# Softmax over rows of 512: the last two rows of the sixth tile's groups are loaded through GpSimd's DMA queue

## The chip, the cores and the metric

The kernel runs on one core of one Trainium2 chip. The metric is the device time in microseconds of an execution; of the kernel before there are three runs, 162.20, 162.28 and 162.33 us, median 162.28.

## The reference

The input x has 16 x 1024 rows of 512 float32 numbers. Each row is divided by a temperature of 0.5 and put through a softmax:

```python
x_scaled = x / temp                         # temp = 0.5
x_max = np.max(x_scaled, axis=-1, keepdims=True)
exp_x = np.exp(x_scaled - x_max)
return (exp_x / np.sum(exp_x, axis=-1, keepdims=True)).astype(np.float32)
```

33.55 MB are read and as many written.

## The kernel before, in words

The 16,384 rows are cut into C = 8 tiles of 128 partitions with G = 16 consecutive rows on each, so a partition's share of a tile is 32 KB, contiguous in HBM and in SBUF. There are six buffers for the tiles (BUFS); tile 6 goes into the buffer of tile 0 and tile 7 into that of tile 1. The exponentials and the products are written over the tile itself.

The order of the work is written out by hand (`manual_schedule`). The lists LOADS, BLOCKS and STORES (lines 38 to 40) say in which pieces a tile is loaded, computed and stored. Tile 0 is loaded in two pieces (four rows and twelve) and computed in three blocks (4, 4 and 8 rows), tile 7 is computed in two blocks of 8, and all others are loaded, computed and stored whole.

For a block, `shift` has VectorE take the negated maximum of each row (L74) and double it (L78): this is the bias. The first `shift` of a tile also calls `load`, which issues the tile's DMAs from Sync (L66). `exponentials` has ScalarE take exp(2x + bias) of each row, with the row's sum beside it (L85). `scale_vector` takes the reciprocals of the sums (L100) and multiplies seven eighths of the rows on VectorE (L102); `scale_scalar` has ScalarE multiply the rest (L111). `store` issues the tile's store from ScalarE's queue (L119).

The loop at the end of the function (L126) runs one block ahead with the exponentials and two with the shifts. So VectorE's order is: reciprocal and product of block i, then maximum and bias of block i + 2. Sync's queue holds all loads in order; the first seven DMAs (tiles 0 to 5) are issued one after the other at the start, and those of tiles 6 and 7 wait for the stores of tiles 0 and 1. The sixth tile, which the change touches, is tile 5: its load is the seventh DMA. GpSimd has nothing to do but four small memsets at the start. The dictionary `biases` holds the bias tile of each block by number: `biases[1]` is that of the second block, rows 4 to 7 of tile 0.

Of the kernel before, what the change touches and what calls it, by code (L numbers as in the profile page):

```python
# [1 line left out]

# [4 lines left out]


@with_exitstack
def kernel(  # L10
    ctx: ExitStack,
    tc: tile.TileContext,
    x: bass.AP,
    out: bass.AP,
):
    nc = tc.nc
    fp32 = mybir.dt.float32
    P = nc.NUM_PARTITIONS
    AX = mybir.AxisListType.X
    EXP = mybir.ActivationFunctionType.Exp  # L20
    COPY = mybir.ActivationFunctionType.Copy
    MAX = mybir.AluOpType.max

    D = x.shape[-1]
    xf = x.flatten_outer_dims()
    of = out.flatten_outer_dims()
    N = xf.shape[0]

    G = 16
    C = N // (P * G)
    assert C * P * G == N
    xr = xf.rearrange("(c p g) d -> c p g d", p=P, g=G)
    outr = of.rearrange("(c p g) d -> c p g d", p=P, g=G)
    WHOLE = [(0, G)]
    LOADS = [[(0, 4), (4, G)]] + [WHOLE] * 7
    BLOCKS = [[(0, 4), (4, 8), (8, G)]] + [WHOLE] * 6 + [[(0, 8), (8, G)]]
    STORES = [WHOLE] * 8  # L40
    BMAX = 16
    BUFS = 6

    data = ctx.enter_context(tc.tile_pool(name="data", bufs=BUFS))
    stats = ctx.enter_context(tc.tile_pool(name="stats", bufs=6))

    ctx.enter_context(tc.manual_schedule())


    warm = stats.tile([P, 1], fp32, name="warm", bufs=1)  # L50
    nc.vector.memset(warm, 0.0)  # L51
    nc.scalar.activation(out=warm, in_=warm, func=EXP)  # L52

    chunks = {}
    blocks = [(c, lo, hi) for c in range(C) for lo, hi in BLOCKS[c]]
    n = len(blocks)
    biases, sums, recips = {}, {}, {}

    def load(c):
        if c < BUFS:  # L60
            chunks[c] = data.tile([P, G, D], fp32, name="xt")
        else:
            chunks[c] = chunks[c - BUFS]
        xt = chunks[c]
        for lo, hi in LOADS[c]:
            nc.sync.dma_start(out=xt[:, lo:hi, :], in_=xr[c][:, lo:hi, :])  # L66

    def shift(i):
        c, lo, hi = blocks[i]
        if c not in chunks:  # L70
            load(c)
        b = hi - lo
        negmax = stats.tile([P, BMAX], fp32, name="negmax")
        nc.vector.tensor_reduce(  # L74
            negmax[:, 0:b], chunks[c][:, lo:hi, :], axis=AX, op=MAX, negate=True
        )
        biases[i] = stats.tile([P, BMAX], fp32, name="bias")
        nc.vector.tensor_scalar_mul(biases[i][:, 0:b], negmax[:, 0:b], 2.0)  # L78

    def exponentials(i):  # L80
        c, lo, hi = blocks[i]
        sums[i] = stats.tile([P, BMAX], fp32, name="sums")
        for g in range(hi - lo):
            row = chunks[c][:, lo + g, :]
            nc.scalar.activation(  # L85
                out=row,
                in_=row,
                func=EXP,
                bias=biases[i][:, g : g + 1],
                scale=2.0,  # L90
                accum_out=sums[i][:, g : g + 1],
            )


    def scale_vector(i):
        c, lo, hi = blocks[i]
        b = hi - lo
        k = b - b // 8
        recips[i] = stats.tile([P, BMAX], fp32, name="recip")
        nc.vector.reciprocal(recips[i][:, 0:b], sums[i][:, 0:b])  # L100
        rows = chunks[c][:, lo : lo + k, :]
        nc.vector.tensor_mul(  # L102
            rows, rows, recips[i][:, 0:k].unsqueeze(2).broadcast_to((P, k, D))
        )

    def scale_scalar(i):
        c, lo, hi = blocks[i]
        b = hi - lo
        for g in range(b - b // 8, b):
            row = chunks[c][:, lo + g, :]  # L110
            nc.scalar.activation(  # L111
                out=row, in_=row, func=COPY, scale=recips[i][:, g : g + 1]
            )

    def store(i):
        c, _, end = blocks[i]
        for lo, hi in STORES[c]:
            if hi == end:
                nc.scalar.dma_start(  # L119
                    out=outr[c][:, lo:hi, :], in_=chunks[c][:, lo:hi, :]  # L120
                )

    shift(0)
    shift(1)
    exponentials(0)
    for i in range(n):  # L126
        if i + 1 < n:
            exponentials(i + 1)
        scale_vector(i)
        scale_scalar(i)  # L130
        if i + 2 < n:
            shift(i + 2)
        store(i)


# [1 line left out]
_INS = ['x']  # L137
_OUTS = [((16, 1024, 512), 'float32')]


# [23 lines left out]
```

## Time and profile before

| what | us |
|---|---|
| median of three runs | 162.28 |
| the profiled execution's own time | 162.34 |
| its span in the profile | 160.57 |
| VectorE busy | 134.6 (84%) |
| ScalarE busy | 102.1 (64%) |
| GpSimd busy | 0.2 |
| loads, share of 16 DMA engines' span | 49.3% |
| stores, share of 16 DMA engines' span | 48.4% |
| the whole tiles' reduction (L74), one | 8.68 |
| the whole tiles' product (L102), one | 7.63 |

The span is what the profiler shows of the execution, from its first instruction to its last; the time holds 1.77 us more around it. A tile's DMA is split over the core's 16 DMA engines; each engine moves eight partitions of it, as packets of up to 32 KB, and posts one packet of 4 bytes when its share is done. A DMA has landed when all sixteen have done so. A line of the page on a queue gives packets, MB and the share of sixteen engines' time; q1 is Sync's queue, q10 ScalarE's, q14 the fetching of instructions.

### The profile page before, as it was taken

What the parts mean: (1) busy time and instruction counts of PE and PEld (TensorE: products, weight loads), DVE (VectorE), ACT (ScalarE), POOL (GpSimd) and SP (SyncE); (2) the same over time, 40 slices, a digit from 0 to 9 for tenths busy, and PEclk for the clock granted to TensorE, in tenths of its full rate; (3) what the DMA queues carried; (4) which work ended last, traced back from release to release, by engine and by line L of the source; (5) the groups of instructions that cost most, each with busy time, mean ns of one, the idle gap of its engine ahead of it and who ended that gap; (6) DMA issues with size and microseconds to landing.
All of it is one profiled execution on the core that took longest, in us unless ns stands there. A gap on an engine that the chain in (4) does not pass through costs nothing.

```text
span 160.6 us, 402 instructions
## 1 busy us (share of the span) xinstructions
DVE 134.6 (84%) x45; ACT 102.1 (64%) x273; POOL 0.2 (0%) x4
## 2 busy tenths in 40 slices
DVE  0507999999999999999999999999999999957000
ACT  3071549069979963998199909991899891790000
POOL 0000000000000000000000000000000000000000
DMA  5999999999999999999999999999999999999993
GB/s 182 471 400 506 400 400 498 408 392 484 424 400 384 400 457 449 400 441 465 400 424 473 408 408 492 400 392 498 416 392 490 424 392 457 457 392 449 465 392 139
DMA packets 2450, 67.13 MB, mean 418 GB/s; under 512 B 272, under 2 KB 272, under 8 KB 272
## 3 DMA queue, kind: packets, MB, share of 16 engines
q1 hardware_dynamic: 1296, 33.56, 49.3%
q10 hardware_dynamic: 1152, 33.55, 48.4%
q14 instruction: 2, 0.02, 0.0%
HBM read 33.55 MB, written 33.55 MB: 418 GB/s over the span
## 4 chain that ended last, share of the span: by engine, by line
DVE 80%; DMA 7%; ACT 4%; issue 0%; SPq 0%
DVE negmax L74 42%; DVE xt L102 36%; DMA xt<-in_x_dram 7%; ACT xt L85 4%; DVE bias L78 1%; DVE recip L100 1%; SPq L66 0%
## 5 line engine op out<-in xcount | busy, mean ns | idle before, releaser
L85 ACT ACTIVATE xt<-xt,bias 128x512 f32<-128x512 f32 x128 | 90.4, 708 | 41.7 <-DVE bias L78 41.2
L74 DVE TENSOR_REDUCE negmax<-xt 128x16 f32<-128x8192 f32 (+2 forms) x11 | 69.9, 6352 | 9.5 <-DMA xt<-in_x_dram 9.5
L102 DVE TENSOR_TENSOR xt<-xt,recip 128x7168 f32<-128x7168 f32 (+2 forms) x11 | 62.0, 5637 | 0.4
L85 ACT ACTIVATION_READ_ACCUMULATOR xt<-xt,bias 128x1 f32 x128 | 23.9, 187 | 0.0
L111 ACT ACTIVATE xt<-xt,recip 128x512 f32<-128x512 f32 x15 | 9.9, 706 | 0.0
L100 DVE RECIPROCAL recip<-sums 128x16 f32<-128x16 f32 (+2 forms) x11 | 2.4, 218 | 1.8 <-ACT xt L85 1.8
L78 DVE TENSOR_SCALAR bias<-negmax 128x16 f32<-128x16 f32 (+2 forms) x11 | 1.9, 173 | 0.4
L52 ACT ACT_TABLE_LOAD x1 | 1.3, 1283 | 0.7 <-PEq L148 0.7
L51 DVE MEMSET warm<- 128x1 f32 x1 | 0.1, 59 | 0.8 <-PEq L148 0.8
L52 ACT ACTIVATE warm<-warm 128x1 f32<-128x1 f32 x1 | 0.2, 203 | 0.0
L148 POOL MEMSET const-bfloat16-1.0<- 128x1 bf16 x1 | 0.1, 103 | 0.0
L148 POOL MEMSET const-uint8-127<- 128x1 uint8 x1 | 0.1, 103 | 0.0
L148 POOL MEMSET const-float32-1.0<- 128x1 f32 x1 | 0.1, 100 | 0.0
L148 POOL MEMSET const-float32-0.0<- 128x1 f32 x1 | 0.1, 99 | 0.2 <-issue 0.2
## 6 DMA issues: line engine op xcount, KB each, us to landing
out_dram<-xt ACTq DMA_DIRECT2D x8, 4096.0 KB, 22.8
xt<-in_x_dram SPq DMA_DIRECT2D x7, 4096.0 KB, 30.2
xt<-in_x_dram SPq DMA_DIRECT2D x1, 3072.0 KB, 11.7
xt<-in_x_dram SPq DMA_DIRECT2D x1, 1024.0 KB, 4.9
```

What stands on the lines that cost most here:

```text
L51: nc.vector.memset(warm, 0.0)
L52: nc.scalar.activation(out=warm, in_=warm, func=EXP)
L74: nc.vector.tensor_reduce(negmax[:, 0:b], chunks[c][:, lo:hi, :], axis=AX, op=MAX, negate=True)
L78: nc.vector.tensor_scalar_mul(biases[i][:, 0:b], negmax[:, 0:b], 2.0)
L85: nc.scalar.activation(out=row, in_=row, func=EXP, bias=biases[i][:, g : g + 1], scale=2.0, accum_out=sums[i][:, g : g + 1],)
L100: nc.vector.reciprocal(recips[i][:, 0:b], sums[i][:, 0:b])
L102: nc.vector.tensor_mul(rows, rows, recips[i][:, 0:k].unsqueeze(2).broadcast_to((P, k, D)))
L111: nc.scalar.activation(out=row, in_=row, func=COPY, scale=recips[i][:, g : g + 1])
L148: nc = _bacc.Bacc("TRN2", target_bir_lowering=False, num_devices=1)
```

## The change

A constant SPLIT = 5 names the sixth tile and TAIL = 2 a number of rows. When `load` comes to that tile, Sync loads rows 0 to 13 of each partition's sixteen. Rows 14 and 15 are loaded by GpSimd, in two DMAs: first partitions 126 and 127, then partitions 0 to 125. The argument `max_dma_last_dim` cuts them into pieces of one row (2 KB). Ahead of the two DMAs, GpSimd copies one column of `biases[1]` into a new small tile `hold`, so its queue stands still until VectorE has written the second block's bias. The buffer, the data and the computation stay as they are.

```diff
@@ tile_softmax_temp_0p5_kernel
     STORES = [WHOLE] * 8
+    SPLIT, TAIL = 5, 2
     BMAX = 16
     BUFS = 6
@@ load
         for lo, hi in LOADS[c]:
+            if c == SPLIT and hi == G:
+                hi = G - TAIL
+                hold = stats.tile([P, 1], fp32, name="hold", bufs=1)
+                nc.gpsimd.tensor_copy(hold, biases[1][:, 0:1])
+                for p0, p1 in ((P - 2, P), (0, P - 2)):
+                    nc.gpsimd.dma_start(
+                        out=xt[p0:p1, hi:G, :],
+                        in_=xr[c][p0:p1, hi:G, :],
+                        max_dma_last_dim=4 * D,
+                    )
             nc.sync.dma_start(out=xt[:, lo:hi, :], in_=xr[c][:, lo:hi, :])
```

## The prediction

> **What bounds the kernel now.** I read the page first: its slices and DMA queues, then its chain of waits.
>
> ```profile
> DVE  0507999999999999999999999999999999957000
> DMA  5999999999999999999999999999999999999993
> ...
> q1 hardware_dynamic: 1296, 33.56, 49.3%
> q10 hardware_dynamic: 1152, 33.55, 48.4%
> q14 instruction: 2, 0.02, 0.0%
> ```
>
> Two resources are full from the second slice on: VectorE up to about 147 us, and the DMA rings up to the end (q1 is Sync's loads, q10 ScalarE's stores: 97.7% of sixteen engines' span). Which one sets the end is read at the last store. The chain of waits, in order of time, ends so (start, us, what):
>
> ```profile
> 133.00 4.34 DVE negmax L74
> ...
> 137.56 5.76 ACT xt L85 x16
> ...
> 143.59 3.89 DVE xt L102
> ```
>
> VectorE is done at 147.48 and ScalarE issues the last store at 147.55; 13 us follow with no engine busy. The single packets in the trace show what they are. Packets of 32 KB follow each other on each engine every 1.21 us without a gap. Store 6 (tile 6) leaves the first engine at 148.35, store 7 starts there at 148.40, and eight packets later, at 148.40 + 8 x 1.21 = 158.08, that engine is done. So VectorE's chain and the DMA backlog meet within 0.05 us on the earliest engine; on all later ones the backlog is what counts. Two questions by window of the DMA queues, 158.1 to 158.6 and 159.2 to 159.5 us:
>
> ```profile
> DMA packets 16, 0.03 MB, mean 66 GB/s; under 512 B 15, under 2 KB 15, under 8 KB 15
> ...
> DMA packets 1, 0.00 MB, mean 0 GB/s; under 512 B 1, under 2 KB 1, under 8 KB 1
> ```
>
> The small packets are the completions, one for each engine. Fifteen engines complete between 158.14 and 158.53; one does at 159.35. The kernel's end waits for one engine, 0.82 us behind the next. Where that engine lost its time is in the window 37 to 39 us:
>
> ```profile
> q1 hardware_dynamic: 29, 0.95, 111.1%
> q14 instruction: 1, 0.01, 1.0%
> ```
>
> An 8 KB fetch of instructions (0.31 us) sits between its load packets, and the packet behind it takes 1.58 us instead of 1.21. At 98.3 the same happens on the same engine, with 1.46. Together 0.31 + 0.37 + 0.31 + 0.25 = 1.24 us, partly regained elsewhere. Last, how a queue enters a saturated engine, by window (us, DVE, ACT, POOL, clock, DMA share, GB/s):
>
> ```profile
> 12.60:45.00 32.40, 31.91 (x13) 20.13 (x57) 0.00 (x0) 1.00 1.01 434
> 45.00:69.00 24.00, 23.86 (x8) 19.16 (x52) 0.00 (x0) 1.00 1.00 418
> 69.00:94.50 25.50, 25.43 (x6) 19.23 (x52) 0.00 (x0) 1.00 1.00 432
> ```
>
> The window in which q10 starts moves 418 instead of about 432 GB/s: (1 - 418/432) x 24 = 0.78 us lost on the average engine, once. The packets that stretch lie between 47 and 50.7 us, up to 0.93 us on an engine.
>
> [...] from 54 us on, packets of q1 and q10 alternate. [...]
>
> **The change part by part.** Packet prices come from the single packets: 32 KB takes 1.213 us and 8 KB 0.309, so a byte costs (1.213 - 0.309)/24576 = 36.8 ps and a packet 0.008 us besides; the completion packets (0.009) fit that. A 2 KB row is then 0.083 us and a 28 KB packet 1.062.
>
> *Sync's tile 5 load* shrinks from sixteen rows to fourteen: each engine has eight packets, 8 x (1.213 - 1.062) = 1.21 us less. No instruction goes.
>
> *GpSimd's DMAs* add, on an engine with nine partitions, 18 x 0.083 + 2 completions x 0.009 = 1.51 us: net +0.30. On an engine with one partition: 2 x 0.083 + 0.018 = 0.18, net -1.02. If spread sixteen ways: 16 x 0.083 + 0.018 = 1.35, net +0.14.
>
> *Entry of a third queue* into engines that are busy with q1. The trace shows entries only for q14 (0.37 and 0.25 us besides the packet itself) and q10 (0.78 mean, 0.93 at most). The bounds are 0 and 0.93: a gain is excluded because the engine has no idle time to fill. I take 0.31, the mean of the two small ones, since nine partitions' rows are 36 KB, nearer to a fetch than to a 4 MB store. If every one of the 18 turns paid 0.31 it would be over 5 us, but the alternation of q1 and q10 at 1.21 us a packet speaks against that.
>
> *The wait.* The copy into hold waits for the second block's bias (row L78 at 15.20, 0.17 us); behind it in GpSimd's queue stand only the two DMAs, and nothing but VectorE's reduction of tile 5 waits for those. That reduction starts at 87.32; the rows are queued from about 17 us and, one in turn beside 32 KB packets, need some 18 x 1.3 = 23 us. Hidden by over 40 us. GpSimd's queue held nothing after 0.7 us, so its instructions cost nothing there. Sync's queue loses nothing: the tile 5 load is issued at 3.79, lands 71.8 us later at 75.6, and the next load waits for store 0 till 69.3.
>
> *What might be late next* is tile 1. Its load lands at 22.57 and VectorE takes it at 24.63: 2.06 us of cover. From 17 to 22.6 there are five turns, so 5 x 0.083 + 0.31 = 0.7 us. Covered; without cover each 0.1 us beyond it goes to VectorE's chain and so to the store at 147.55.
>
> *VectorE* gets at most two more waits at 87.4 (20 to 30 ns each, as Sync's semaphore waits) [...] hidden on engines whose backlog reaches past 148.4 and small beside the rest.
>
> *Sum.* An engine with nine partitions gets +0.30 + 0.31 = +0.61, one of the two relieved -1.02 + 0.31 = -0.71. So everything hangs on which engine is the late one. The records name the queue of a packet but not its engine. The one hint is the first load: the late engine's first packet starts at 1.82, fifth of the sixteen; [...] but the first five lie within 0.09 us. I take it as not relieved: its end moves from 159.35 to 159.96. Profiled execution: 162.34 + 0.61 = 162.95, span 160.57 + 0.61 = 161.18. Against the median of the runs, 0.06 lower: 162.28 + 0.61 = 162.89.
>
> **The rivals.**
>
> *Relieved, and entry cheap* (the other side). If the late engine is one of the two, it ends at 159.35 - 1.02 + entry = 158.4, the next latest at 158.53 + 0.30 + entry = 158.83, and this sets the end: 0.52 us less, 161.76 with entry at nothing. For: two rows are 1.02 us of work, about the size of the lag. Against: the fifth place, and the other spread. It decides as long as the entry stays under 0.2 us; then the gain is over 0.32 us.
>
> *Relieved, but entry dear.* With 0.31 to 0.93 the next latest ends at 159.14 to 159.76: -0.21 to +0.41 us, 162.07 to 162.69, middle 162.3. For: both kinds of entry in the trace cost something.
>
> *Tile 1 late, or each turn paid for.* Five turns at 0.31 + 0.083 are 2.0 us, the whole cover of 2.06; and eighteen such turns load each engine with some 5 us. 163.6 to 168. Against: the alternation above.
>
> *Spread sixteen ways with a cheap entry*: +0.14 us on the late engine, 162.42, not to be told from before.
>
> **How the numbers follow.** Not relieved, at +0.3 to +1.24 us: 0.45, nearly all slower. Relieved and cheap: 0.22. Relieved and dear: 0.18, mostly within the bound. Each turn paid: 0.08. Sixteen ways, cheap: 0.07. About 0.2% (0.32 us) is what a measurement here can tell from no change. Faster: 0.21 + 0.03 = 0.24. Same: 0.04 + 0.13 + 0.07 + 0.01 = 0.25. Slower: 0.41 + 0.02 + 0.08 = 0.51. The range runs from the relieved case with free entry, 161.76, to the unrelieved one with the dearest, 162.28 + 0.30 + 0.93 = 163.51, a little widened for the turns: 161.75 to 163.6. The likeliest case's own range is 162.6 to 163.5.
>
> **What would show it.** The late engine's completion against the other fifteen, at the last store: still one straggler about 0.8 us behind means not relieved; all sixteen within 0.5 us means relieved. The fifteen others' completions move by net bytes and entry: 158.53 to about 159.1 with mine. GB/s between 17 and 50 us tells the entry's price. VectorE's last multiply should still end within 0.2 us of 147.48; if it does not, tile 1 or tile 5 was late, and my step on the cover is wrong. The prediction is wrong as a whole if the straggler is gone, or if the GpSimd queue's packets run beside q1's at no cost.

## The result, and the profile after

The changed kernel takes 163.36 us (median of 4 runs, 163.23 to 163.60) against 162.24 us for the kernel before in the same session (median of 4): a ratio of 1.0071, 95% interval 1.0053 to 1.0088. That is 1.1 us slower. The profiled execution took 163.23 us with a span of 161.45, so 1.78 us lie around the span, as before; it was the fastest of the four.

The page after has the same picture, with one more queue, q0, which is GpSimd's:

```profile
DVE  0608999999999999999999999999999999955000
DMA  5999999999999998999999999999999999999993
...
q1 hardware_dynamic: 1296, 33.03, 48.9%
q10 hardware_dynamic: 1152, 33.55, 48.2%
q0 software_dynamic: 192, 0.52, 0.9%
q14 instruction: 2, 0.02, 0.0%
```

q10's 1152 packets are eight stores of 128 data packets and sixteen completions each. Of q0's 192, 128 carry the rows, 4 KB each, which is two rows in one packet.

VectorE's chain has not moved. The chain of waits, in order of time, ends with the same product, and it is over at 147.34 us (147.48 before):

```profile
143.45 3.89 DVE xt L117
```

So the loss is in the DMA queues. The completions of the last store, asked by window of the queues (158.4 to 158.7, then 159.3 to 160 us), show two things at once:

```profile
DMA packets 6, 0.16 MB, mean 546 GB/s; under 512 B 1, under 2 KB 1, under 8 KB 1
...
DMA packets 15, 0.00 MB, mean 0 GB/s; under 512 B 15, under 2 KB 15, under 8 KB 15
```

One engine completes in the first window, at 158.53, and fifteen in the second, from 159.37 to 159.89. The straggler of before is gone: nobody is alone at the end any more. But the whole field has come to it, and passed it: the last completion is at 159.89 against 159.35.

Where the field lost its time is seen by window of the engines' work (us, DVE, ACT, POOL, clock, DMA share, GB/s), here from 20.5 to 34.5 us, while GpSimd's rows are in flight, and from 47 to 50.7, where ScalarE's first store enters. The kernel before:

```profile
20.50:34.50 14.00, 13.86 (x8) 6.70 (x19) 0.00 (x0) 1.00 1.04 447
47.00:50.70 3.70, 3.70 (x1) 3.70 (x13) 0.00 (x0) 1.00 1.13 399
```

and the changed one:

```profile
20.50:34.50 14.00, 13.86 (x8) 6.89 (x19) 0.00 (x0) 1.00 1.01 378
47.00:50.70 3.70, 3.70 (x1) 3.70 (x12) 0.00 (x0) 1.00 1.05 452
```

In the first stretch 378 GB/s are moved in place of 447. In the single packets, a 32 KB packet of Sync's takes 1.40 us there on average instead of 1.21; from 22 to 33 us every one of them is stretched (1.42 on average), so it happens on every engine, the relieved ones too. I call this the slow phase. Its size below is the sum over the packets of what each took beyond the prices of the prediction, divided by sixteen: 1.91 us for each engine between 18 and 36 us (0.00 before). In return the 0.79 us that the entry of the stores cost before, at 45 to 53 us, is 0.01 after.

GpSimd's own side is as it was meant (timeline of GpSimd; start, us):

```profile
15.24 0.18 POOL L74 COPY hold<-bias 128x1 f32<-128x1 f32 x1 [14.79 <-DVE bias L93]
15.36 1.48 POOL L76 DMA_DIRECT2D xt<-in_x_dram  x2
```

The copy waits for the bias at 15.2 us, and the two DMAs follow at once. The first row moves only at 20.61, over 5 us after the first issue; the rows are in by 35 us and wanted at 87.

The span is 0.88 us longer. The last completion accounts for 0.54, and the closing for 0.35: from the last completion to the end of the span there are 1.56 us, and 1.21 before. Sync waits there for four semaphores one after the other, 0.06 us each, where before it waited for one, and GpSimd's closing instructions take 0.08 us more in all. The 0.88 us are what the two profiled executions differ by. The medians differ by 1.12: the profiled execution was 0.13 us under its kernel's median, that of before 0.10 above its own, and no trace shows the rest.

### The profile page after: what moved, and what is told of

Same layout as the page of the kernel before. It is cut to its first block, busy times and chain, and to the rows that moved or that the text cites. A ratio compares the mean times of both kernels' runs of the same rounds, so it can differ in the third digit from the quotient of the medians.

```text
span 161.4 us, 409 instructions
## 1 busy us (share of the span) xinstructions
DVE 134.6 (83%) x45; ACT 102.1 (63%) x273; POOL 1.8 (1%) x7
## 3 DMA queue, kind: packets, MB, share of 16 engines
q1 hardware_dynamic: 1296, 33.03, 48.9%
q10 hardware_dynamic: 1152, 33.55, 48.2%
## 4 chain that ended last, share of the span: by engine, by line
DVE 75%; DMA 7%; issue 5%; ACT 4%; SPq 0%; DVEq 0%
DVE negmax L89 42%; DVE xt L117 31%; DMA xt<-in_x_dram 7%; ACT xt L100 4%; DVE bias L93 1%; DVE recip L115 1%; SPq L81 0%; DVEq L93 0%
## 5 line engine op out<-in xcount | busy, mean ns | idle before, releaser
L76 POOL DMA_DIRECT2D xt<-in_x_dram x2 | 1.5, 740 | 0.0
```

The lines of the kernel that those rows point to most:

```text
L76: nc.gpsimd.dma_start(out=xt[p0:p1, hi:G, :], in_=xr[c][p0:p1, hi:G, :], max_dma_last_dim=4 * D,)
```

## The experiments

Each kernel was timed in turn with the kernel before, whose medians in these sessions were 162.27 to 162.32 us; the ratios below are to those.

**The other order.**

```diff
-                for p0, p1 in ((P - 2, P), (0, P - 2)):
+                for p0, p1 in ((0, P - 2), (P - 2, P)):
```

> The changed kernel with GpSimd's two DMAs in the other order: partitions 0 to 125 first, then 126 and 127. Theory A ([...]): the relieved engines become two others, the straggler is back. Last store: fourteen engines complete near 159.4 to 159.9 as in the changed kernel, one about 0.8 us later near 160.6, two near 158.5; time about 0.7 us over the changed kernel's 163.36, so 164.1. Theory B (the order decides nothing, GpSimd's data are spread sixteen ways or the straggler went for another reason): 163.4, completions as in the changed kernel.

163.48 us, ratio 1.0073 (1.0058 to 1.0088). The completions of the last store, 158.2 to 159.7 and 160 to 160.6 us:

```profile
DMA packets 17, 0.07 MB, mean 44 GB/s; under 512 B 15, under 2 KB 15, under 8 KB 15
...
DMA packets 1, 0.00 MB, mean 0 GB/s; under 512 B 1, under 2 KB 1, under 8 KB 1
```

Two engines complete at 158.24 and 158.26, thirteen from 158.86 to 159.60, and one at 160.31, 0.71 us behind the next. The straggler is back, so the order decides who is relieved, and with two partitions first it is relieved: theory A. An engine can be followed from the end of each packet to the start of the next (not every link is unique). In this profile the engine with both instruction fetches then carries nine of GpSimd's 4 KB packets and ends last, at 160.31; in a kernel further down (late), with two partitions first, it carries one and ends at 158.60. Two engines stand apart from fourteen here, by 0.60 us and more, which the sixteen-way spread would not give. The time, though, is 0.6 us under what A said. In the profile the slow phase is 0.47 us shorter (1.44 us for each engine, against 1.91), which is most of it; why it is shorter is open. By time alone the two orders can't be told apart here (163.36 and 163.48, four runs each); the packets tell them apart, and on a store, below, so do the times.

**One DMA of 128 partitions.**

```diff
-                for p0, p1 in ((P - 2, P), (0, P - 2)):
+                for p0, p1 in ((0, P),):
```

> The changed kernel with GpSimd's two rows loaded by one DMA of 128 partitions. Each engine then has eight rows' packets, none is relieved. Theory A (what costs is the slow stretch of Sync's packets while GpSimd's rows are in flight, about 0.2 us a packet): eight slow packets, the fifteen engines complete near 159.5, the one with the fetches 0.8 us later near 160.3, time 163.8 to 164.0. Theory B (the two-step split itself, with two DMAs' completions, costs): back to 162.5 to 162.9.

162.58 us, ratio 1.0014 (1.0004 to 1.0024): theory B, and my theory A fell. The windows, as above:

```profile
20.50:34.50 14.00, 13.86 (x8) 6.75 (x19) 0.00 (x0) 1.00 1.05 449
47.00:50.70 3.70, 3.70 (x1) 3.70 (x13) 0.00 (x0) 1.00 1.01 337
```

GpSimd's rows are in flight in the first window as before, on 128 packets of 4 KB, and nothing slows: 449 GB/s, Sync's packets at 1.22. The stores' entry costs its share again (0.88 us). So it is neither GpSimd's queue, nor small rows in turn with large packets.

**The rows from ScalarE's queue, whole and split.** Both kernels load tiles 1 to 5 from Sync ahead of the loop's first shift, tile 5 with fourteen rows (an edit of LOADS, not shown), and leave GpSimd out.

```diff
     for i in range(n):
         if i + 1 < n:
             exponentials(i + 1)
+        if i == 0:
+            ...
+            nc.scalar.dma_start(
+                out=chunks[5][:, G - 2 : G, :], in_=xr[5][:, G - 2 : G, :]
+            )
```

> The same two rows of tile 5 are loaded by one 128-partition DMA issued from ScalarE's queue at about 18 us, after the first two blocks' exponentials; GpSimd has nothing to do. Theory A (4 KB rows in turn with Sync's 32 KB packets slow all engines, whoever issues them): Sync's packets take about 1.4 us instead of 1.21 for eight rounds and the end is some 1.1 us later than before, about 163.4 to 163.9 with the straggler. Theory B ([...]): no stretch beyond the 0.8 us that a second queue's entry costs once, and this is then not paid at 47 us; time 162.2 to 162.5.

162.50 us, ratio 1.0008 (1.0002 to 1.0015), no slow phase (0.01 us):

```profile
20.50:34.50 14.00, 13.86 (x8) 6.85 (x19) 0.00 (x0) 1.00 1.04 445
```

This is theory B's time, but not its account. B had the 0.8 us paid at 18 us and not at 47; they were still paid at 47 (0.74 us), though ScalarE's queue had moved its rows from 19.2 us on. And B's reading, that GpSimd's path is what slows, is taken away by one128, which is GpSimd's path without a slow phase, and by the next kernel:

```diff
-            nc.scalar.dma_start(
-                out=chunks[5][:, G - 2 : G, :], in_=xr[5][:, G - 2 : G, :]
-            )
+            for p0, p1 in ((P - 2, P), (0, P - 2)):
+                nc.scalar.dma_start(
+                    out=chunks[5][p0:p1, G - 2 : G, :],
+                    in_=xr[5][p0:p1, G - 2 : G, :],
+                )
```

> As acttail, two rows of tile 5 loaded from ScalarE's queue at about 18 us, but in two DMAs, partitions 126 and 127 and then 0 to 125. Theory A (what stretches Sync's packets is that fourteen engines carry 126 partitions, so that a partition's rows are written by another engine than the one that writes the rest of it): Sync's packets take about 1.4 us for nine rounds whoever issues the rows. [...] the straggler stays: end about 1.2 to 1.5 us later than in acttail, 163.6 to 164.1. Theory B (only GpSimd's queue does it): no stretch, 162.5 to 162.9.

163.74 us, ratio 1.0080 (1.0060 to 1.0101): theory A. The windows of the split one:

```profile
20.50:34.50 14.00, 13.86 (x8) 6.92 (x19) 0.00 (x0) 1.00 1.03 398
47.00:50.70 3.70, 3.70 (x1) 3.70 (x11) 0.00 (x0) 1.00 0.99 425
```

The slow phase is there (398 GB/s, 1.57 us for each engine) with no GpSimd in it, and the loss at 47 us is gone with it. q10 has 1296 packets, 144 more than before: 128 of rows, and sixteen completions for the two DMAs together. The relief fell on two other engines: completions at 158.07 and 158.09, the straggler at 160.52, 0.91 us behind the next.

**Another cut.**

```diff
-                for p0, p1 in ((P - 2, P), (0, P - 2)):
+                for p0, p1 in ((P - 16, P), (0, P - 16)):
```

> The changed kernel with its two GpSimd DMAs cut at partition 112 instead of 126: 16 partitions first, then 112. Both numbers divide by sixteen, so every engine should get one partition and seven, none is relieved. Theory A (rows on other engines than the rest of their partitions): stretch of Sync's packets to about 1.4 us for seven rounds, fifteen completions near 159.4, the straggler near 160.1, time 163.4 to 163.9. Theory B (the unequal fourteen-engine load itself): no stretch, as one128, 162.5.

164.15 us, ratio 1.0108 (1.0083 to 1.0132): theory A, a little above its range. The windows:

```profile
20.50:34.50 14.00, 13.86 (x8) 6.88 (x19) 0.00 (x0) 1.00 1.06 408
47.00:50.70 3.70, 3.70 (x1) 3.70 (x12) 0.00 (x0) 1.00 0.99 425
```

q0 has 160 packets: 128 of rows and 32 completions, twice the sixteen that one128 has in its 144. Nobody is relieved (fifteen completions up to 159.52, the straggler at 160.33), and the slow phase is 1.53 us. The unequal load of fourteen engines is not its cause either.

**The rows from elsewhere in HBM.** One128 with another source.

```diff
-                        in_=xr[c][p0:p1, hi:G, :],
+                        in_=xf[(c * P + 40) * G : ((c + 1) * P + 40) * G, :].rearrange(
+                            "(p g) d -> p g d", g=G
+                        )[:, hi:G, :],
```

> As one128, one GpSimd DMA of 128 partitions for the last two rows of tile 5, but the rows are read from 40 partitions further on in HBM (so tile 5's last two rows are other rows of x; the amount and the SBUF side stay). Theory A (the stretch comes on the SBUF side, when another engine writes a partition's rows): no stretch between 18 and 36 us, 162.4 to 162.7 as one128. Theory B (it comes on the HBM side, from which rows an engine reads): stretch by 0.2 us a packet, 163.4 to 164.2.

It fills tile 5 with rows that don't belong there, so its output is not the softmax of x; the bytes moved are the same.

```profile
20.50:34.50 14.00, 13.86 (x8) 6.91 (x19) 0.00 (x0) 1.00 1.04 444
```

162.55 us, ratio 1.0015 (1.0007 to 1.0023), 0.08 us of excess: theory A. Rows read from 40 partitions further on in HBM are not slowed. What the runs show is the cut: cut at 126 or at 112, the early rows cost 1.44 to 1.91 us for each engine (the changed kernel, swap, act126, pool112), and in DMAs of 128 partitions 0.01 and 0.08 (acttail, shift40).

I read it as the SBUF side. An engine with nine partitions of GpSimd's rows, as followed in swap, and eight of Sync's load writes at least one partition whose other rows another engine writes. That this is what slows is argued, not shown: the records name neither the engine nor the partition of a packet, and for the cut at 112 the packet counts don't imply it. Nor is it the only reading left, because this kernel shifts all reads alike, while the cut also groups them in another way; and two loads in place of one were not tried apart from the cut. So the cut is shown as the cause, and the mechanism below it is not.

**A small DMA alone.** The kernel before, and two rows of two partitions loaded once more by GpSimd into a spare tile.

```diff
+        if c == 5:
+            ...
+            nc.gpsimd.tensor_copy(hold, biases[1][:, 0:1])
+            extra = stats.tile([P, 2, D], fp32, name="extra", bufs=1)
+            nc.gpsimd.dma_start(
+                out=extra[P - 2 : P], in_=xr[c][P - 2 : P, G - 2 : G, :],
+                max_dma_last_dim=4 * D,
+            )
```

> The kernel before, Sync's loads as they were; in addition GpSimd waits for the second block's bias and loads two rows of two partitions (8 KB in all) once more into a small spare tile that nobody reads. Theory A (the entry of any second queue costs 0.8 us once, and the change only pays it earlier): after 20 us the packets stretch for about 0.8 us in all, at 47 us they do not, time 162.3 to 162.5. Theory B (each queue pays its own entry): stretch at 20 and again at 47, time 162.8 to 163.2. Theory C (so small a DMA costs nothing): stretch at 47 only, as before, 162.3.

162.57 us, ratio 1.0019 (1.0011 to 1.0027). The packets are those of theory C: nothing at 20 us (0.01 us), 0.84 at 47, last completion 159.43. Yet the kernel is 0.25 us slower, and the closing shows it: 1.43 us from the last completion to the end, in place of 1.21. So a second queue has no price of entry as such, and GpSimd's one small DMA costs about 0.2 us at the end. Not all of that is GpSimd's: Sync waits for two semaphores more than before, 0.12 us. In act126, where GpSimd issues nothing, the closing is 1.35 us, with the same two waits more.

**GpSimd's rows after the stores' entry.**

```diff
-                nc.gpsimd.tensor_copy(hold, biases[1][:, 0:1])
+                nc.gpsimd.tensor_copy(hold, biases[4][:, 0:1])
```

> The changed kernel with GpSimd held until the bias of tile 2 (block 4, about 46 us) instead of the second block's, so that its rows come after ScalarE's first store has entered at 45 to 50 us. Theory A (the 0.8 us that the entry of the stores costs is a slack that any slow phase uses up once): 0.8 us of stretch near 47, then 1.1 us with GpSimd's rows, 1.9 in all as in the changed kernel, time 163.2 to 163.6. Theory B (the early rows happened to shift the engines so that the stores' entry was free): 0.8 and then 1.9 us, time 164.0 to 164.5. Theory C (beside stores the wrong-engine rows do not slow anything): 0.8 only, and with the straggler relieved 162.2 to 162.5.

162.68 us, ratio 1.0021 (1.0011 to 1.0030): between theories A and C, and neither of them. The windows from 50.7 to 76 us, before and here:

```profile
50.70:76.00 25.30, 25.23 (x6) 20.91 (x57) 0.00 (x0) 1.00 1.00 430
```

```profile
50.70:76.00 25.30, 25.23 (x6) 20.86 (x56) 0.00 (x0) 1.00 1.00 421
```

The entry costs 0.77 us, and then the rows cost another 0.6 us for each engine, a third of the 1.91 of the early ones. The straggler is gone (completions from 158.16 to 159.32). Of the 0.59 us, 0.54 fell on Sync's loads; ScalarE's 32 KB stores, in turn with them on the same engines, took 1.216 us on average. What slows is thus the loads. They write SBUF, which fits my reading above; but they also read HBM, so it doesn't settle it.

**The same relief on a store.** Loads as before; the last two rows of tile 6 are stored in two steps by GpSimd, the rest by ScalarE.

```diff
             if hi == end:
+                if c == 6:
+                    hi = G - 2
+                    for p0, p1 in ((P - 2, P), (0, P - 2)):
+                        nc.gpsimd.dma_start(
+                            out=outr[c][p0:p1, hi:G, :],
+                            in_=chunks[c][p0:p1, hi:G, :],
+                            max_dma_last_dim=4 * D,
+                        )
                 nc.scalar.dma_start(
```

> The kernel before with its loads, but the last two rows of each partition of tile 6 are stored by GpSimd in the same two steps, two partitions and then 126, when the tile is done (about 134 us); ScalarE stores the other fourteen rows. Theory A ([...] rows read from SBUF by another engine than the rest do not slow the stores): fifteen completions near 158.7 at the latest, the straggler gone, last completion about 158.8 and the end 0.35 us later for GpSimd's share of the closing: 161.9 to 162.2. Theory B (reading is slowed as writing is): stretch of ScalarE's packets by 0.2 us for nine rounds, 163.3 to 164.

161.99 us, ratio 0.9980 (0.9969 to 0.9990), 22 runs: faster than both kernels. The completions of the last store, 158.1 to 158.9 and 158.9 to 159.3 us:

```profile
DMA packets 15, 0.00 MB, mean 0 GB/s; under 512 B 15, under 2 KB 15, under 8 KB 15
...
DMA packets 1, 0.00 MB, mean 0 GB/s; under 512 B 1, under 2 KB 1, under 8 KB 1
```

The last one stands at 159.04 and the next at 158.85. No packet is slowed while GpSimd's rows leave (0.01 us): the same cut on a store costs nothing measurable here. The profiled execution, at 162.33 us, was among the slowest of this kernel, and its span equals that of before; the gain rests on the timings. The order was tested here too:

```diff
-                    for p0, p1 in ((P - 2, P), (0, P - 2)):
+                    for p0, p1 in ((0, P - 2), (P - 2, P)):
```

> store6 with the two GpSimd stores in the other order, 126 partitions first. Theory A (store6 gains by relieving the engine with the fetches): the straggler is back, at 159.35 + 0.28 = 159.6 against the others' 158.8, time 162.5 to 162.7. Theory B (store6 gains in another way): 162.0 as store6.

162.76 us, ratio 1.0032 (1.0020 to 1.0043). Completions, 158.1 to 158.9 and 159.3 to 159.8 us:

```profile
DMA packets 16, 0.03 MB, mean 41 GB/s; under 512 B 15, under 2 KB 15, under 8 KB 15
...
DMA packets 1, 0.00 MB, mean 0 GB/s; under 512 B 1, under 2 KB 1, under 8 KB 1
```

The straggler is back at 159.58, where A put it. The two differ in one line, and in 0.77 us (medians of two sessions, in which the kernel before had 162.27 and 162.31).

**Two variants of it.** With `if c == 7`, the last store itself:

> As store6, with tile 7, the last store. GpSimd issues two DMAs after 147.5 us, one behind the other (0.70 and 0.78 us in the changed kernel), and its first row followed the issue by 5 us there, so the rows start near 153 and have to end with the backlog near 158. Theory A: the straggler is gone and the rows fit in, 161.9 to 162.3. Theory B: GpSimd's rows are the last to land, one turn at a time, 163 to 166.

162.44 us, ratio 1.0009 (1.0000 to 1.0018). ScalarE's packets are all done by 158.34, but GpSimd's rows, issued after 147.5, go on till 159.32 and land last: neither a gain nor theory B's loss. Here the split store is not free: after 148 us the packets take 0.29 us more than their prices for each engine, two thirds of it on GpSimd's own rows (0.184 us each on average, 0.159 in store6). With `hi = G - 1` in store6, one row in place of two:

> store6 with one row in place of two. The relief halves to about 0.5 us, the other engines' extra to 0.14. If the end is set by the latest of the two groups: straggler 159.35 - 0.5 = 158.85, others 158.53 + 0.14 = 158.67, last completion 158.85 against store6's 159.04: 161.8 to 162.1. If GpSimd's rows cost by the turn rather than by the byte (nine turns as before): 162.1 to 162.4.

162.66 us, ratio 1.0021 (1.0011 to 1.0031), over both expectations. The straggler stayed at 159.50, the others ended by 158.42. GpSimd's bytes went as 63 packets of 4 KB and two of 2 KB here. Followed as above, from the end of a packet to the start of the next, each of the sixteen engines carries three to five of them, the one with the fetches four. So these rows were shared by all, and nobody was relieved; that the DMAs are dealt out otherwise with one row is read from the packets, and the reason is open.

## Why the prediction was right or wrong

**Right.** The DMA backlog sets the end, in the kernel before through one engine that the instruction fetches delay (159.35, the next at 158.53); VectorE's chain and the waits on tile 1 and tile 5 stayed covered (the last product ends 0.14 us earlier, not later). Slower was forecast, by 0.61 us, and the time lies in the range. The size is short: the median moved by 1.12. That the direction came out is in good part luck. The 0.61 was +0.30 of bytes on the late engine, which was relieved instead, and +0.31 for an entry that wasn't paid; the prediction itself named a vanished straggler as the sign of being wrong as a whole, and it vanished.

**Wrong: "I take it as not relieved".** The straggler was relieved. In the changed kernel it is lost among the fifteen, and turning the order of the two DMAs brings it back, on the load side and on the store side. The hint of the first load's order, fifth of sixteen, misled: that this place tells which engines two partitions go to was my assumption and is shown by no run, and the first five lay within 0.09 us, too close to carry it. The nine partitions on an engine and the one, too, were assumed then; the packets of swap and of late show them. Nearest to what came is the rival "relieved, but entry dear", whose highest last completion was 159.76; measured, 159.89. Its times, up to 162.69, were too low all the same, by 0.67 us. (Two slips of the sums carry nothing: a relieved engine's 158.4 is 158.33 ahead of any entry, and the middle of that rival's times is 162.4, not 162.3.)

**Wrong: "entry of a third queue", 0.31 us.** There was no entry price: tiny and one128 enter and pay nothing. In its place stood the slow phase, 1.91 us, of which 0.78 came back because the stores' entry at 47 us was then free. It is not a price of each turn either, since one128 takes its turns at 1.22 us a packet; nor is it confined to the engines with many rows. No term of the prediction priced the cut. With the measured terms, an engine with nine partitions gets 9 x 0.159 + 0.04 - 1.21 + 1.91 - 0.78 = +1.39 us (the trace has packets of 4 KB, two rows each, not the pieces of one row that I described, eighteen of which I priced; the sum is nearly the same). The field moved from a mean of about 158.3 to about 159.6, by 1.3. One of the relieved engines gets 0.18 - 1.21 + 1.91 - 0.78 = +0.1, and one completes at 158.53, in the upper end of where the field was; the other, the straggler, would come to about 159.45 by the same sum, which is among the fifteen.

**Missing: the closing.** I priced nothing after the last landing; it is 0.35 us longer in the changed kernel, and 0.22 with one small DMA of GpSimd's. Of these, 0.18 and 0.12 are Sync's additional waits for semaphores, which any further DMAs to wait for can bring (act126: 0.14 in all, without GpSimd).

**Open.** Why the stores' entry costs 0.7 to 1.0 us in ten kernels and nothing in the four that had an early slow phase (the changed one, swap, act126, pool112) isn't settled. Late pays both, 0.77 and 0.6, so it isn't a slack that is simply used up first. "Entry" may be the wrong word: in the kernel before, the packets that stretch are all Sync's, and of the 0.79 us 0.77 fall ahead of the store's first packet, which starts at 49.64. In the changed kernel, which pays nothing, that packet starts at 48.83.

## What to carry to other kernels

Where the last packets leave one DMA engine alone at the end, look for who delays it before moving bytes; a few rows sent over other engines can relieve it, and the order of two DMAs decides which (store6 and store6swap, 161.99 and 162.76 us). Do that on a store, early enough to be done before the last one: the same uneven cut on a load slowed all sixteen engines for as long as it ran (1.91 us for each in the changed kernel), and cost more than the straggler. Of the three stores tried with two partitions first, only store6 gained, 0.3 us. And count the closing: one more small DMA to wait for has a price at the end, here 0.2 us, a quarter of what the relief could bring.

## What the runs showed of the hardware that was not expected

- A load of 128 partitions and one cut at 126 or 112 are not alike while another load streams: Sync's 32 KB packets took 1.21 to 1.22 us on average beside the first and 1.35 to 1.40 beside the others (20.5 to 34.5 us), issued from GpSimd or from ScalarE, and on all engines at once. Later, beside stores, the loads were slowed and the stores were not (0.54 and 0.03 us for each engine, late). With the same cut on a store nothing was slowed in store6 (0.01 us), and 0.29 us in store7.
- When the first store came to engines that are full of loads, 0.7 to 1.0 us for each engine was lost, once, in ten kernels, and nothing in four; it was lost on Sync's packets, ahead of the store's first.
- In the changed kernel GpSimd's first row moved 5.2 us after its DMA was issued (15.36 to 20.61).
